# A hand-written order for four engines in branch A, gate copies staged in the weight tiles, and feed-forward weight sums issued after a result

## The chip, the cores and the metric

The kernel runs on one core of one Trainium2 chip. The metric is the device time of one execution in microseconds; a kernel's time is the median over its runs, and one more execution is recorded by the hardware profiler. TensorE does the matrix products (PE in the profile, PEld for its weight loads), VectorE is DVE, ScalarE is ACT, GpSimd is POOL and SyncE is SP, the engine that issues the transfers in the kernel before.

## The reference, cut to what matters

One encoder block over 1024 tokens and 16 meta tokens of width 1024, in float32. Branch A is differential attention (4 heads, two score maps each, over all 1040 keys), branch B is windowed attention; both are multiplied by a sigmoid gate, added, projected, and followed by a SwiGLU feed-forward.

```python
def diff_attn_rows(q1, q2, k1, k2, v, qpos, kpos, key_real, slopes, lam):
    ...
    s1 = jnp.einsum('bqhd,bkhd->bhqk', q1, k1).astype(jnp.float32) * scale + bias
    s2 = jnp.einsum('bqhd,bkhd->bhqk', q2, k2).astype(jnp.float32) * scale + bias
    attn = jax.nn.softmax(s1, axis=-1) - lam * jax.nn.softmax(s2, axis=-1)
    return jnp.einsum('bhqk,bkhe->bqhe', attn.astype(v.dtype), v)
...
    merged = jax.nn.sigmoid(ga) * (y_a @ w_ba) + jax.nn.sigmoid(gb) * (y_b @ w_bb)
    return merged @ w_o

def swiglu(h, w_gate, w_up, w_down):
    return (jax.nn.silu(h @ w_gate) * (h @ w_up)) @ w_down
```

## The kernel before, in words

**Products.** Every float32 product is made of three products of split operands: the operand is copied to a rounded high part (ACT, L113) and the rest is kept as a low part (L114, on DVE or POOL); TensorE then does high times high, high times low, low times high. The gates' projections, the output projection and the feed-forward are also done in seven block products instead of eight (blocks 1 to 7, `p` in the code), which takes sums of weight blocks and of results.

**The stage of branch A** (from 325 to 638 us). The outer loop at L926 runs over 32 tiles, `n`: 4 heads `h` of 8 tiles `t` of 128 queries. One tile's work is:

- `scores_a` (L813): for each of the two maps (m = 1, then 0) three chunks of keys (392, 392 and 256). TensorE makes the chunk in a PSUM bank (L829), DVE adds the distance bias and carries the running minimum (L832). After the third chunk ACT takes the exponential of the whole row and its sum (L837); DVE then takes a reciprocal (m = 1, L839) or a product of scalars (m = 0, L841), joins the two maps (L843) and copies 32 columns (L844).
- `transpose_a` (L847), for the tile before (T_LAG is 1): three groups of transposes (L855), each read by ACT (high part, L858) and DVE (low part, L859).
- `values_a` (L862) and `normed_a` (L872): the product with the values for each pair of tiles, and a norm for every four tiles.
- Between these, single steps of the gates' projection: `gate_steps` (L729) holds 50 products of four steps each, three matmuls a step (L738). A product's weights are loaded (`g_load`, L620) and split (`g_split`, ACT L113 and POOL L114). Its result goes from PSUM to DRAM: 26 products are copied by ACT to a staging tile (`gate_stage`, L746, two buffers), 24 (p in 1, 6, 7) are added by DVE to an earlier partial result that was loaded into a tile `gk` (L632, L743, three buffers). The store is L747.
- POOL forms sums of the output projection's weights (`wo_ahead`, L785), with loads and stores on SP.

Score chunks and transposes share five PSUM banks (tag "sc", SC = 5) in turn, the gate products two (PP2). The string `SLOTS` gives TensorE's order within a tile: s is a chunk of scores, g a gate step, t a group of transposes, n a step of values or norm. At the start of heads 1 to 3 ten gate steps stand together (G_HEAD), at the very start four, and 30 (HOLD) are kept for the end.

Inside `tc.manual_schedule(engines=...)` the named engines run instructions in the order in which the code writes them. In this stage only TensorE stands in such a block; the order of ACT, DVE, POOL and SP is chosen by the compiler's planner, which simulates the timeline beforehand. Once the program is built, each of these queues is fixed and runs in order.

**The feed-forward's first half** (from 808 to 1234 us). TensorE and DVE are in written order. A product `product_f` (L1456) is 12 matmuls (L1466). `prepare` (L1206) splits weights ahead of time, up to eight operand tiles; for block 6 the weights first need three sums on DVE (`weights`, L1247 to L1249). Results leave PSUM by ACT copies (L1486, L1489) or DVE operations (L1475, L1480, L1482). Four banks serve each of gate (i = 0) and up (i = 1) products; a product whose bank is still unread waits. `turn_f` (L1330) transposes the normed tokens and forms token sums (L1355 to L1358); `low_of` issues low parts that were put off (L1524).

Of the kernel before, what the change touches and what calls it, by code (L numbers as in the profile page):

```python
# [27 lines left out]
AH = 4  # L28
# [8 lines left out]
N_WAIT = 3  # L37
PP2 = 2
# [3 lines left out]
G_BUFS = 2  # L42
# [27 lines left out]
def encoder_block(ctx: ExitStack, tc: tile.TileContext, x, meta, norm_mix, w_in, lq1, lk1, lq2, lk2,  # L70
# [544 lines left out]
    def g_load(n, raw=None):  # L615
# [4 lines left out]
        nc.sync.dma_start(raw, ws_d[k][:, (5, 6, 7, 3).index(p)] if p in (5, 6, 7, 3) else  # L620
# [3 lines left out]
    def g_split(n, op=None):  # L624
# [9 lines left out]
    g_done = [0, 0]  # L634

    def g_ahead(n):
# [25 lines left out]
    def load_a0(h, q, k):  # L662
        q[0] = apool.tile([P, S], F32R, tag="q0", name=f"aq{h}_0")
        nc.sync.dma_start(f32(q[0]), qa_d[h][0])
        if h:
            load_k(h, 0, k[0])
            return q, k, load_v(h)
# [60 lines left out]

    def gate_steps():  # L729
        for n, (p, k) in enumerate(order_g):  # L730
            g_ahead(n + 1)
            op, act = g_ready.pop((p, k)), G_ACT[p]
# [3 lines left out]
            for c in range(4):  # L736
                for i, (a, b) in enumerate(((0, 0), (0, 1), (1, 0))):
                    nc.tensor.matmul(ps, op[:, a, c], quad(b, *act)[:, c], start=(p in (2, 5, 1) and c == 0 and i == 0),  # L738
                                     stop=(p in (2, 3, 4) and c == 3 and i == 2), skip_group_check=True)
                if c == 3:  # L740
                    if p in (1, 6, 7):
                        st = g_kept.pop((p, k))
                        nc.vector.tensor_tensor(st, ps, st, ALU.add)  # L743
                    else:
                        st = gpool.tile([P, 512], F32, tag="g", name="gate_stage", bufs=G_BUFS)
                        nc.scalar.copy(st, ps)  # L746
                    nc.sync.dma_start(g_place(p, k), st)  # L747
                    if (p, k) in ((5, 3), (5, 7), (3, 7)):
                        later_p = {(5, 3): 6, (5, 7): 7, (3, 7): 4}[p, k]
                        load_sums(later_p, *G_ACT[later_p])  # L750
# [9 lines left out]
    ld = *ld, load_v(0)  # L760
# [4 lines left out]
    prepool, close_pre = pool("prepool")  # L765
    wo_d = {(p, c): dram.tile([P, 512], F32, name=f"wo_d{p}_{c}") for p in (5, 6, 7, 3) for c in range(4)}
# [14 lines left out]
    def wo_ahead(n):  # L781
# [4 lines left out]
        nc.sync.dma_start(wo_d[(7, 5, 6, 3)[i], c], out)  # L786
# [26 lines left out]
    def scores_a(h, t, ld, s):  # L813
        slope = 2.0 ** -(2 * (h + 1))
        qs, ks, _ = ld
# [6 lines left out]
        u0 = 896 - t * P  # L822
        for m in (1, 0):
# [13 lines left out]
            nc.scalar.activation(s[m][:, 0:L], s[m][:, 0:L], AF.Exp, bias=low, scale=-1.0, accum_out=sum_of[m])  # L837
# [869 lines left out]
```

## Time and profile before

| | |
|---|---|
| median of 3 runs | 1450.66 us (1448.5 to 1454.46) |
| profiled execution: time, span | 1453.61 us, 1451.8 us |
| PE busy | 1419.5 us (98%) |
| PEld busy | 1216.4 us (84%) |
| DVE busy | 943.4 us (65%) |
| ACT busy | 696.0 us (48%) |
| POOL busy | 627.2 us (43%) |
| mean granted TensorE clock | 0.993 |

A row of a group of instructions gives line, engine, operation, the tiles it writes and reads, its shape and count, then busy time and the mean duration of one, then the engine's idle time just before such instructions and what ended it. A row of the timeline gives start and duration in us; in brackets is the engine's idle time before it and what ended that. A row of stages gives the length of a stretch, each engine's busy time in it with the count of instructions, the granted TensorE clock, the busy share of the DMA engines and GB/s. Matmuls overlap in their pipeline, so that one lasts longer than the distance to the next.

### The profile page before, as it was taken

What the parts mean: (1) busy time and instruction counts of PE and PEld (TensorE: products, weight loads), DVE (VectorE), ACT (ScalarE), POOL (GpSimd) and SP (SyncE); (2) the same over time, 40 slices, a digit from 0 to 9 for tenths busy, and PEclk for the clock granted to TensorE, in tenths of its full rate; (3) what the DMA queues carried; (4) which work ended last, traced back from release to release, by engine and by line L of the source; (5) the groups of instructions that cost most, each with busy time, mean ns of one, the idle gap of its engine ahead of it and who ended that gap; (6) DMA issues with size and microseconds to landing.
All of it is one profiled execution on the core that took longest, in us unless ns stands there. A gap on an engine that the chain in (4) does not pass through costs nothing. (4 is left out here: it accounts for less than half of the span.)

```text
span 1451.8 us, 21189 instructions
## 1 busy us (share of the span) xinstructions
PE 1419.5 (98%) x7231; PEld 1216.4 (84%) x7231; DVE 943.4 (65%) x1680; ACT 696.0 (48%) x1315; POOL 627.2 (43%) x593
## 2 busy tenths in 40 slices
PE   8999999998999899999999999999999999999997
PEld 7998989987888889888888878888888888888886
DVE  7478535637778788733876896554455554787567
ACT  6366535545555455555445633333333333444454
POOL 4599126743532122245144565454445452000444
PEclk9999999999999999999999999999999999999999
DMA  8467668988768564569522624333333333964443
GB/s 242 88 210 239 191 164 269 277 287 290 250 221 257 175 196 155 167 209 330 201 80 88 189 87 150 119 109 105 100 96 107 103 103 105 316 223 139 124 130 139
DMA packets 195804, 255.00 MB, mean 176 GB/s; under 512 B 18976, under 2 KB 116704, under 8 KB 195696
## 3 DMA queue, kind: packets, MB, share of 16 engines
q1 hardware_dynamic: 195696, 253.65, 55.6%
q8 instruction: 57, 0.93, 0.3%
q14 instruction: 51, 0.42, 0.1%
HBM read 165.84 MB, written 81.20 MB: 170 GB/s over the span
## 5 line engine op out<-in xcount | busy, mean ns | idle before, releaser
L114 POOL TENSOR_TENSOR wop<-wf,wop 128x512 fp32r<-128x512 f32 x128 | 175.1, 1372 | 167.8 <-ACT wop L113 155.3
L1466 PE MATMUL pg<-t,wop 128*128 128x512 f32 x1056 | 242.6, 389 | 0.0
L1466 PEld LDWEIGHTS pg<-t,wop 128*128 128x128 f32 x1056 | 198.3, 188 | 41.1
L1582 PE MATMUL pd<-ob,oa 128*128 128x512 f32 x924 | 210.4, 389 | 0.5 <-POOL oa L114 0.4
L1582 PEld LDWEIGHTS pd<-ob,oa 128*128 128x128 f32 x924 | 173.2, 188 | 37.6 <-POOL oa L114 0.9
L1466 PE MATMUL pg<-b,wop 128*128 128x512 f32 x792 | 185.2, 392 | 2.8 <-DVE copies_p L1480 2.8
L1466 PEld LDWEIGHTS pg<-b,wop 128*128 128x128 f32 x792 | 149.5, 189 | 34.2 <-DVE copies_p L1480 3.2
L738 PE MATMUL pg<-hT_hi,gop 128*128 128x512 f32 x384 | 144.4, 400 | 0.4 <-DVE gk L743 0.4
L114 POOL TENSOR_TENSOR gop<-gr,gop 128x512 fp32r<-128x512 f32 x47 | 64.4, 1373 | 165.7 <-ACT gop L113 161.3
L113 ACT ACTIVATE wop<-wf 128x512 fp32r<-128x512 f32 x128 | 80.1, 631 | 84.1 <-PE pg L1466 48.0
L114 POOL TENSOR_TENSOR oa<-ra,oa 128x512 fp32r<-128x512 f32 x33 | 44.1, 1337 | 170.6 <-ACT oa L113 169.2
L113 ACT ACTIVATE oa<-ra 128x512 fp32r<-128x512 f32 x77 | 48.7, 632 | 105.1 <-PE pd L1582 44.0
L837 ACT ACTIVATE as<-as,amn 128x1040 f32<-128x1040 f32 x64 | 74.5, 1164 | 49.9 <-DVE amn L832 41.4
L829 PE MATMUL aps<-ak,aq 128*128 128x392 f32 (+1 forms) x384 | 91.0, 331 | 7.1 <-DVE amn L832 6.2
L1247 DVE TENSOR_TENSOR s<-wf,wf 128x512 f32<-128x512 f32 x22 | 22.3, 1011 | 103.4 <-DMA wf<-in_w_ff_up_dram 52.3
L829 PEld LDWEIGHTS aps<-ak,aq 128*128 128x128 f32 x384 | 70.4, 192 | 21.0 <-DVE amn L832 7.5
L738 PEld LDWEIGHTS pg<-hT_hi,gop 128*128 128x128 f32 x384 | 73.3, 191 | 12.2 <-DVE gk L743 1.1
L339 POOL TENSOR_SCALAR bs<-bs,bdn 128x432 f32<-128x432 f32 (+1 forms) x64 | 41.4, 664 | 86.6 <-DVE bdn L337 74.3
L738 PE MATMUL pg<-hT_lo,gop 128*128 128x512 f32 x192 | 76.5, 398 | 0.0
L114 POOL TENSOR_TENSOR woh<-wo,woh 128x512 fp32r<-128x512 f32 x28 | 38.5, 1378 | 67.4 <-ACT woh L113 66.3
L329 DVE CUSTOM_DVE_ANT_0 bs<-bps,tbx,nsink 128x432 f32<-128x432 f32 (+1 forms) x64 | 38.2, 622 | 38.5 <-PE bps L327 29.3
L832 DVE CUSTOM_DVE_ANT_0 as<-aps,dist,far_a 128x392 f32<-128x392 f32 x64 | 39.6, 619 | 30.2 <-PE aps L829 29.7
(311 smaller groups left out, 3219.2 us busy)
## 6 DMA issues: line engine op xcount, KB each, us to landing
ra<-aop SPq DMA_DIRECT2D x77, 256.0 KB, 2.7
wf<-in_w_ff_gate_dram SPq DMA_DIRECT2D x24, 512.0 KB, 4.0
wf<-in_w_ff_up_dram SPq DMA_DIRECT2D x24, 512.0 KB, 3.9
aop<-as SPq DMA_DIRECT2D x44, 256.0 KB, 2.1
w_c<-in_w_in_dram SPq DMA_DIRECT2D x17, 512.0 KB, 5.9
aop<-c SPq DMA_DIRECT2D x33, 256.0 KB, 2.0
ts_d<-to SPq DMA_DIRECT2D x16, 512.0 KB, 3.6
gw<-in_w_in_dram SPq DMA_DIRECT2D x32, 256.0 KB, 4.2
```

Source lines behind the costliest of these rows:

```text
L113: nc.scalar.activation(hi, src, AF.Copy)
L114: lo_eng.tensor_tensor(lo, src, f32(hi), ALU.subtract)
L329: nc.vector.tensor_tensor_reduce(st[:, r, :W], ps[:, :W], tb, 2.0 ** -(4 * g + r + 1), nsink[:, 4 * g + r:4 * g + r + 1], ALU.add, ALU.min ...
L339: nc.gpsimd.tensor_scalar(st[:, r, :W], st[:, r, :W], dn[:, r:r + 1], 1.0, ALU.mult, ALU.mult)
L738: nc.tensor.matmul(ps, op[:, a, c], quad(b, *act)[:, c], start=(p in (2, 5, 1) and c == 0 and i == 0), stop=(p in (2, 3, 4) and c == 3 and ...
L829: nc.tensor.matmul(ps[:, :n], qs[m][:, t * P:(t + 1) * P], ks[m][:, vv, k0:k0 + n], start=(vv == 0), stop=(vv == 1))
L832: nc.vector.tensor_tensor_reduce(s[m][:, k0:k0 + n], ps[:, :n], far_by, slope, low, ALU.add, ALU.min, mn[:, m, i:i + 1])
L837: nc.scalar.activation(s[m][:, 0:L], s[m][:, 0:L], AF.Exp, bias=low, scale=-1.0, accum_out=sum_of[m])
L1247: tt(s1, a21, a22, ALU.add)
L1466: nc.tensor.matmul(ps, op[:, x, c, :], b[:, y, c, :], start=(p in (1, 2, 5) and c == 0 and n == 0), stop=(p in (4, 2, 3) and c == 3 and n ...
L1582: nc.tensor.matmul(ps[u], oa[:, a, u * P:(u + 1) * P], ob[:, b, :], start=(p in (1, 2, 5) and j == 0 and k == 0), stop=(p in (2, 3, 4) and ...
```

## The change

In branch A the loop is put inside a second `manual_schedule`, for ACT, DVE, POOL and SP, and the pieces of a tile's work are taken apart so that each stands at a written place:

- `exp_a`, `scale_a` and `join_a` are the exponentials, the reciprocal and the join, taken out of `scores_a`. The exponential of map 1 stands after the third chunk; that of map 0 after the first group of transposes (EXP_AT = 1). The join of a tile stands after the first chunk of the next tile; the copy of 32 columns and two of the three low parts of the transposes are put off (`behind`, `catch_up`) to just after that join and the second chunk.
- Splits of gate weights are put in a list (`held_back`) and let go one at a time (`let_go`) after the fifth chunk and after the third group of transposes.
- A gate result is not written at once: `settle` and `store_gates` issue it after the third or the sixth chunk, or at the second step of the next product. Stores of gate results and loads of gate weights are issued by ACT's queue (`nc.scalar.dma_start`) instead of SP's.
- Partial gate results are loaded by `ask_kept`, up to three ahead, apart from the splits.
- The staging tiles have three buffers (G_BUFS) in another pool, the first shares the tag "w", and the last two products' copies use weight tiles (tag "gr"). `yg` has one buffer instead of two.
- The next head's queries and keys are asked for in the last tile of a head, its values in its third tile.
- Tile 1 has two more gate steps; the loop's total count of gate steps is the same. `fill(1000)` is called before three pools are closed instead of after.

In the feed-forward `prepare` is not called before products 4 to 7 (it was: before 6 and 7), and is called right after product 7's results. In `turn_f` one token sum is formed from an ACT copy of a PSUM bank and the other PSUM bank instead of from two tiles in SBUF.

The diff, cut to its core:

```diff
-G_BUFS = 2
+G_BUFS = 3
...
-        nc.sync.dma_start(raw, ws_d[k][:, (5, 6, 7, 3).index(p)] if p in (5, 6, 7, 3) else
+        (nc.sync if held_back is None else nc.scalar).dma_start(raw, ws_d[k][:, (5, 6, 7, 3).index(p)] if p in (5, 6, 7, 3) else
...
         if p in (1, 6, 7):
-            kept = g_kept[p, k] = gpool.tile([P, 512], F32, tag="gk", name=f"gk{p}_{k}", bufs=GK_BUFS)
-            nc.sync.dma_start(kept, g_place(p, k))
+            kept_to_do.append((p, k))
+    def ask_kept():
+        while kept_to_do and len(g_kept) < GK_BUFS:
+            load_kept()
...
             while g_done[i] < min(n + far, len(order_g)):
-                what(g_done[i])
+                if i and held_back is not None:
+                    held_back.append(g_done[i])
+                else:
+                    what(g_done[i])
                 g_done[i] += 1
+    def let_go(n):
+        while n > 0 and held_back:
+            g_split(held_back.pop(0))
+            n -= 1
...
+    def gate_result(p, k, ps):
+        if p in (1, 6, 7):
+            while (p, k) not in g_kept:
+                load_kept()
+            st = g_kept.pop((p, k))
+            nc.vector.tensor_tensor(st, ps, st, ALU.add)
+        else:
+            tag, bufs = ("w", 2) if (p, k) == order_g[0] else ("g", G_BUFS)
+            if (p, k) in order_g[-2:]:
+                st = gpool.tile([P, 512], F32, tag="gr", name=f"gate_stage{p}_{k}", bufs=GR_BUFS)
+            else:
+                st = prepool.tile([P, 512], F32, tag=tag, name=f"gate_stage{p}_{k}", bufs=bufs)
+            nc.scalar.copy(st, ps)
+        to_store.append((p, k, st))
...
+    def store_gates():
+        while to_store:
+            p, k, st = to_store.pop(0)
+            nc.scalar.dma_start(g_place(p, k), st)
+    def settle(store=True):
+        while owed:
+            gate_result(*owed.pop(0))
+        if store:
+            store_gates()
...
+                if c == 1 or burst[0]:
+                    settle()
+                if c == 1:
+                    ask_kept()
                 if c == 3:
...
+                    owed.append((p, k, ps))
...
+    def exp_a(s, m):
+        sum_of, dn = s["of"]
+        nc.scalar.activation(s[m][:, 0:L], s[m][:, 0:L], AF.Exp, bias=s["low", m], scale=-1.0, accum_out=sum_of[m])
...
+        behind[1:1] = [lambda: nc.vector.tensor_copy(s[0][:, L:L + 2 * NM].rearrange("p (a k) -> p a k", a=2),
+                                                     s[0][:, S:L].unsqueeze(1).broadcast_to([P, 2, NM]))]
...
+    order_av = tc.manual_schedule(engines={mybir.EngineType.Activation, mybir.EngineType.DVE, mybir.EngineType.Pool, mybir.EngineType.SP})
+    order_av.__enter__()
...
+        for what in SLOTS if n != 1 else "sgsgsngsgssggtntnt":
+            if what == "s" and n < AH * NT:
+                next(scoring)
+                scored += 1
+                if scored == 1 and n:
+                    join_a(tiles[n - 1][2])
+                    catch_up(1)
+                if scored == 2:
+                    catch_up(9)
+                if scored == 3:
+                    exp_a(s, 1)
+                    settle()
+                    if t == NT - 1 and h < AH - 1:
+                        ask_kept()
+                        ahead = load_a1(h + 1)
+                    if n == 0:
+                        let_go(1)
+                if scored == 4 and t in (3, 4, 5, 6):
+                    wo_ahead(4 * h + t - 3)
+                if scored == 5:
+                    scale_a(t, s)
+                    if n:
+                        let_go(1)
+                if scored == 6:
+                    settle(False)
+                if scored == 6 and n == 0:
+                    exp_a(s, 0)
+                    store_gates()
+                if scored == 6 and t == NT - 1 and h < AH - 1:
+                    ahead = load_a0(h + 1, *ahead)
+            elif what == "t" and n:
+                next(turning)
+                turned += 1
+                if turned == EXP_AT and n < AH * NT:
+                    exp_a(s, 0)
+                    store_gates()
+                if turned == 3:
+                    let_go(1)
...
-        nc.vector.tensor_tensor(left, t2, left, ALU.subtract)
+        nc.scalar.copy(left, pts[1])
+        nc.vector.tensor_tensor(left, left, pts[0], ALU.subtract)
...
-        if n not in (4, 5):
+        if n not in range(4, 8):
             prepare()
...
         product_f(*steps[n][1])
         used[0] -= 1
+        if n == 7:
+            prepare()
         low_of(2)
```

More of the change, by code (lines that the diff above doesn't have):

```diff
@@ L37 @@
 N_WAIT = 3
+EXP_AT = 1
 PP2 = 2
@@ L739, in gate_steps @@
                                      stop=(p in (2, 3, 4) and c == 3 and i == 2), skip_group_check=True)
+                if c == 1 or burst[0]:
+                    settle()
+                if c == 1:
+                    ask_kept()
                 if c == 3:
[L741 to L750, printed above, removed]
+                    owed.append((p, k, ps))
+                    if n == len(order_g) - 1:
+                        settle()
                 yield
@@ L978, in encoder_block @@
     close_pre()
+    fill(1000)
     close_apool3()
```

108 lines of the change are left out of this document (72 added, 36 removed).

## The prediction

> **What bounds the kernel now.** I read the page's busy times first, then the stages, then TensorE's waits in the two stages that the change touches, then the stretches at a lower clock.
>
> ```profile
> span 1451.8 us, 21189 instructions
> PE 1419.5 (98%) x7231; PEld 1216.4 (84%) x7231; DVE 943.4 (65%) x1680; ACT 696.0 (48%) x1315; POOL 627.2 (43%) x593
> ```
> ```profile
> 325.00:638.40 313.40, 298.59 (x1768) 266.52 (x1767) 239.41 (x664) 173.21 (x324) 97.68 (x77) 0.98 0.64 210
> ...
> 808.40:1233.80 425.40, 422.64 (x1868) 349.81 (x1866) 254.93 (x280) 165.93 (x288) 215.94 (x156) 1.00 0.36 113
> ```
> ```profile
> PE aps L829 <- DVE amn L832: 6.2, 4, 2.2
> PE apt L855 <- DVE as L843: 4.4, 5, 2.0
> ```
> ```profile
> PE pg L1466 <- DVE copies_p L1480: 2.8, 1, 2.8
> ```
> ```profile
> 341.38:344.80 3.42, 3.42 (x13) 3.13 (x12) 3.27 (x14) 2.58 (x6) 2.74 (x3) 0.50 1.07 405
> ...
> 843.14:846.55 3.41, 3.32 (x8) 2.65 (x9) 3.41 (x4) 1.49 (x3) 3.41 (x3) 0.50 0.00 0
> ```
>
> TensorE bounds the kernel: it is busy 98% of the span, and the change adds and removes no matmul. So all that can be won is TensorE's own idle time. In the stage of branch A (first row of stages) that is 313.40 - 298.59 = 14.8 us, most of it behind DVE: score chunks that wait for a bank DVE has not read, and transposes that wait for the join. In the feed-forward's first half it is 425.40 - 422.64 = 2.8 us, one single wait for a bank (L1480). The last fence holds the first and last of four stretches with a granted clock of 0.50, each 3.41 or 3.42 us long; three lie in branch A and one in the feed-forward, each at or behind the end of a long wait. Half a clock for 3.42 us costs 1.7 us of work, so 5.1 us and 1.7 us. What the change could win at most is 14.8 + 5.1 = 19.9 us in branch A and 2.8 + 1.7 = 4.5 us in the feed-forward: 24.4 us, or 1.7%.
>
> Here a rule and the trace differ. The Trainium skill ("TensorE: Matmul & The Clock Gate", section "Why this matters for your kernels") says that idle gaps beyond about 3 us put the clock back to half. The longest waits here are 2.2, 2.0 and 2.8 us (last column of the three rows of waits), and yet half clock followed. By the page's rule the 6.8 us would have some other cause and stay; that case is among the rivals.
>
> **Branch A: what blocks, and what the written order does to it.**
>
> ```profile
> 336.24 0.16 DVE L839 RECIPROCAL adn<-adn 128x1 f32<-128x1 f32 x1 [4.48 <-ACT as L837]
> ```
> ```profile
> 403.38 0.59 ACT L746 COPY gate_stage<-pg 128x512 f32<-128x512 f32 x1 [3.46 <-DMA g_d<-gate_stage]
> ```
> ```profile
> 405.15 0.16 DVE L839 RECIPROCAL adn<-adn 128x1 f32<-128x1 f32 x1 [3.75 <-ACT as L837]
> ...
> 406.05 0.48 DVE L832 CUSTOM_DVE_ANT_0 as<-aps,dist_m,amn 128x256 f32<-128x256 f32 x1
> ```
> ```profile
> 479.27 0.69 DVE L743 TENSOR_TENSOR gk<-pg,gk 128x512 f32<-128x512 f32 x1 [2.18 <-DMA gk<-g_d]
> ```
>
> Each of the three clock losses has a queue that stood still. At 336.24 DVE waited 4.48 us for an exponential, at 405.15 it waited 3.75 us for one, because ACT's queue held a gate copy in front that waited 3.46 us for a store to free its staging tile. At 479.27 DVE stood 2.18 us in front of a partial gate result that had not been loaded. DVE's score chunks stood behind each, and TensorE behind those. The change puts the exponential of map 1 ahead of the gate copy and of the split, gives staging three buffers, and asks for partial results up to three ahead. I cost these three blocks at nothing afterwards: the cover is a store or load that now has three products (three tiles, some 22 us) to land. In the ten gate steps ahead of a head three products take only about 8 us; if a load misses there, DVE stands about 2 us as at 479.27.
>
> What comes in their place is a chain. In the written order these stand in line, each behind the one before on its engine or for its data: the last chunk of map 1 on DVE, the exponential on ACT, a split, the high part of the first transposes, the second exponential, then on DVE the scalar product, the join, a low part, a chunk, the 32-column copy, another low part, and the last chunk of map 1 of the next tile. The planner could put other work between; now one turn of this loop is the least time of a tile.
>
> ```profile
> 488.27 1.16 ACT L837 ACTIVATE as<-as,amn 128x1040 f32<-128x1040 f32 x1 [0.28 <-DVE amn L832]
> 489.34 0.19 ACT L837 ACTIVATION_READ_ACCUMULATOR as<-as,amn 128x1 f32 x1
> 489.43 0.58 ACT L858 ACTIVATE at<-apt 128x512 fp32r<-128x512 f32 x1
> 489.90 0.59 ACT L875 ACTIVATE ysq<-apy 128x512 f32<-128x512 f32 x1
> ...
> 493.93 0.58 ACT L746 COPY gate_stage<-pg 128x512 f32<-128x512 f32 x1 [2.69 <-PE pg L738]
> 494.41 0.63 ACT L113 ACTIVATE gop<-gr 128x512 fp32r<-128x512 f32 x1
> 494.94 1.15 ACT L837 ACTIVATE as<-as,amn 128x1040 f32<-128x1040 f32 x1
> ```
> ```profile
> 489.56 0.27 DVE L841 TENSOR_SCALAR adn<-adn,neglam,as 128x1 f32<-128x1 f32 x1 [0.72 <-ACT as L837]
> 489.86 1.30 DVE L843 SCALAR_TENSOR_TENSOR as<-as,adn,as 128x1040 f32<-128x1040 f32 x1
> 491.08 0.62 DVE L832 CUSTOM_DVE_ANT_0 as<-aps,dist,far_a 128x392 f32<-128x392 f32 x1
> 491.63 0.08 DVE L832 DVE_READ_ACCUMULATOR2_ANT amn<- 128x1 f32 x1
> 491.63 0.69 DVE L859 TENSOR_TENSOR at<-apt,at 128x512 fp32r<-128x512 f32 x1
> 492.23 0.17 DVE L844 COPY as<-as 128x32 f32<-128x32 f32 x1
> 492.31 0.27 DVE L859 TENSOR_TENSOR at<-apt,at 16x128 fp32r<-16x128 f32 x1
> 492.51 0.60 DVE L832 CUSTOM_DVE_ANT_0 as<-aps,dist,amn 128x392 f32<-128x392 f32 x1
> ```
> ```profile
> 489.50:526.20 36.70, 13.97 (x60) 10.80 (x60) 16.62 (x30) 1.00 0.39 126
> ```
>
> From start to start in these rows: last chunk 0.48 (the row at 406.05), exponential 1.16, split 0.53, high part 0.47, second exponential to scalar product 1.29, scalar product 0.30, join 1.22, chunk 0.55, low part 0.60, copy 0.08, low part 0.20: 6.88 us. The norm's three small DVE instructions, once in four tiles and each at most a low part's 0.60, add up to 0.4 a tile: 7.3 us. Where the gate result is an ACT copy (0.48 in the rows), 7.8 us. Against it stands TensorE's own pace: the last row counts the score matmuls of a stretch with hardly a wait, 60 at 12 a tile, so 5 tiles in 36.7 us or 7.34 us a tile. DVE-gate tiles fit, tiles with an ACT copy miss by 0.4 us.
>
> The issue of transfers on ACT has no row, since ACT issues none before. SP's rows for the same store take this:
>
> ```profile
> 494.54 0.34 SPq L747 DMA_DIRECT2D g_d<-gate_stage  x1
> ```
>
> The lower bound is nothing (the queue issues while ACT works, and SP's shorter queue even helps). The upper bound is a store and a load at 0.34 each, behind the full 0.58 of the copy instead of 0.48: 0.8 us a tile, where both stand between the two exponentials. By the written positions that is so in heads 0 and 2, where a product ends at a tile's second gate step; after the ten extra steps of heads 1 and 3 it ends at the fourth, and the store falls behind the second exponential.
>
> The tiles: with ACT copies 6 in head 0, 5 in head 1, and a quarter of 14 in heads 2 and 3 (products of block 4), 14.5 in all. Lower end 14.5 x 0.42 = 6 us. Upper end: head 0 6 x 1.2 = 7.2, head 1 2.1, head 2 (a quarter at 1.2, the rest at 0.2) 2.9, head 3 0.7: 13 us. I take the middle, 9.5 us, because half of the tiles stand where the issue has no cover. Refilling the chain in tiles 0 and 1 and behind each head I put at 2.5 us (four times about the 0.6 us of one low part that arrives late). Sum for branch A: 19.9 goes, 12 comes, 7.9 us won. Single waits of the new kind are around a microsecond, under the 2 us and more behind which this trace lost clock.
>
> Other moved steps: the loads of the next head go out in the last tile, some 5 us sooner on SP, but behind `ask_kept`, which may hold SP for a store's landing; the values go out two tiles later and are wanted a tile after that. Stores and weight loads leave SP, so nothing of SP's queue is lengthened. The `wo` sums and norms are in POOL's queue between splits; POOL is busy 98 of 313 us here and covers them. The two extra gate steps in tile 1 come off the end: no matmul more. `fill(1000)` and the pools' closing move no instruction of TensorE.
>
> **The feed-forward.**
>
> ```profile
> 836.10 0.68 DVE L1247 TENSOR_TENSOR s<-wf,wf 128x512 f32<-128x512 f32 x1
> ...
> 839.71 1.65 DVE L1249 TENSOR_TENSOR wf<-s,wf 128x512 f32<-128x512 f32 x1
> 841.29 1.28 DVE L1524 TENSOR_TENSOR t<-ts,t 128x512 fp32r<-128x512 f32 x2
> 842.49 0.68 DVE L1480 TENSOR_TENSOR copies_p<-pg,copies_p 128x512 f32<-128x512 f32 x1
> ```
>
> Six sums run on DVE from 836.10 to 841.29, and product 7's result (L1480), for whose bank TensorE waits, runs behind them at 842.49. Without them in front it runs at about 842.49 - 5.2 = 837.3; the bank is wanted at 843.23 - 2.76 = 840.5. So this wait and its clock loss go. Next in line are the sums themselves: behind L1480 and L1482 (at most another 1.65) they begin at about 839.6, the first three end near 841.7, and ACT and POOL need 0.6 and 1.3 for the split: 843.6, when product 12 wants it one product (2.7 us) behind 840.5, at 843.2, and its low part 0.4 later. The second block of three is as tight. I leave 1.2 us there, so 3.3 of 4.5 us are won; the ends are 0 and 4.5. The ACT copy in `turn_f` is 4 x 0.6 us on an engine with room; DVE's part loses one SBUF operand, which I count as nothing.
>
> **The sum.** 7.9 + 3.3 = 11.2 us. The profiled execution took 1453.61 us, 1.8 beyond its span; it would take 1442.4. It lies 2.95 us above the median of 1450.66, so the median would be 1439.5. I say 1440.
>
> **Rivals.**
>
> 1. Nearly all is won: ACT's issue is free and the chain has slack, so that 4 us stay in branch A and none in the feed-forward. 1450.7 - 15.9 - 4.5 = 1430. For it: DVE stands still no longer than these blocks. Against: the sum of the chain.
> 2. The wait only changes its place: upper end of the chain (13), 5 us of refilling at four heads, and the weight sums late by as much as they gain (1 us won). 1450.7 - 1.9 - 1 = 1448. The page's rule on the clock lands here too: with the 6.8 us left in place 4.4 us are won, 1446; four half-clock stretches behind four waits speak against it, chance 0.02, counted in this case.
> 3. Slower. The store and the load on ACT's queue cost their 0.8 us in every tile, with the copy's 0.42, because in-order ACT stands at each issue wherever it is written: 31 x 1.2 = 37 us come, 19.9 + 3.3 go, 1465. It decides from 0.98 us a tile on (30 us against the 23 won and 7 of the bound). Against it: half of the stores stand behind the second exponential, off the chain, and DVE's gates need no copy.
>
> **How the numbers follow.** About 0.5%, 7 us, is what a measurement of this kernel can tell from no change. My forecast has 0.45, rival 1 0.15, rival 2 0.28, rival 3 0.12. Faster is the first two, 0.60; same 0.28; slower 0.12. The range runs from just below rival 1 to beyond rival 2, 1428 to 1453, and leaves out rival 3 and a little on either side. The forecast's own range, 6 to 13 us in the chain and 0 to 4.5 in the feed-forward, is 1435 to 1446.
>
> **What would show it.** In TensorE's waits of branch A the three long ones and their half-clock stretches are gone; what is left is many waits of 0.3 to 1.2 us on DVE, more in head 0 than in head 3. ACT's exponential of map 1 starts within 0.1 us of its chunk, and the wait before the scalar product L841 ("ACT as") grows, since DVE now stands for the second exponential. In the feed-forward L1480 of product 7 runs ahead of L1247, and the 2.8 us wait is gone or is a shorter one for a split weight. I am wrong if ACT's issues show as gaps between the two exponentials in all tiles (rival 3), if a new wait near 2 us halves the clock again, or if a head's first chunk waits for its keys behind `ask_kept`.

## The result: about 1% slower

The changed kernel takes 1466.52 us (median of 9 runs, 1460.58 to 1472.29) against 1450.7 us for the kernel before (median of 9 runs on the same chip, the three shown among them). The ratio is 1.0097, 95% interval 1.0073 to 1.0122. The forecast was 1440, with 1453 as the upper end of the range; what came is on the other side. The profiled execution was the fastest of the nine, 1460.58 us.

The page's busy times (span 1458.8 us, 21151 instructions), then the two stretches at half clock, and branch A and the feed-forward's first half as rows of stages (columns as in the prediction):

```profile
PE 1420.5 (97%) x7231; PEld 1210.3 (83%) x7231; DVE 934.4 (64%) x1680; ACT 693.4 (48%) x1319; POOL 630.3 (43%) x593
```
```profile
831.71:835.12 3.41, 3.41 (x9) 2.63 (x8) 3.31 (x5) 1.46 (x3) 3.41 (x3) 0.50 0.47 161
473.31:483.55 10.24, 5.34 (x15) 4.24 (x16) 2.03 (x6) 1.33 (x4) 2.51 (x2) 0.50 0.42 135
323.10:643.70 320.60, 301.56 (x1769) 262.24 (x1768) 234.12 (x664) 168.57 (x324) 100.91 (x77) 0.98 0.63 204
815.10:1240.70 425.60, 422.68 (x1865) 349.75 (x1866) 251.91 (x279) 166.81 (x289) 213.89 (x156) 1.00 0.36 113
```

TensorE does the same 7231 matmuls. Branch A takes 320.60 us where it took 313.40, and TensorE's idle time in it is 19.0 us where it was 14.8. The feed-forward has not changed (425.60 against 425.40), so the step that was to win 3.3 us there won nothing. In this execution the three half-clock stretches of branch A are gone, as forecast, but one of 10.24 us has come, in which TensorE works 5.34 us; at half clock that is 2.7 us lost. TensorE's waits in the two stages (who waited for whom: total us, times, longest):

```profile
PE aps L888 <- DVE at L934: 8.0, 11, 1.2
PE pg L790 <- ACT gop L114: 6.8, 1, 6.8
...
PE pg L790 <- ACT gate_stage L762: 1.9, 1, 1.9
...
PE aps L888 <- DVE amn L891: 1.5, 4, 0.5
```
```profile
PE pg L1593 <- DVE kept L1484: 2.9, 1, 2.9
PE pg L1593 <- ACT kept L1483: 1.2, 1, 1.2
```

The first row is the chain of the prediction, many waits of up to 1.2 us behind low parts (L934). The second is new and single: the gate product at the start of head 2 waits 6.8 us for a split of its weights. The third is of the same kind, at head 1: a gate product waits 1.9 us for ACT to copy an earlier result out of its bank. The last two are the feed-forward's: the wait for L1480 is gone and the edit in `turn_f` has put two others in its place.

What stood behind the 6.8 us is read from ACT's, DVE's and SP's queues in that place (time line; ACTq and SPq rows are issues of transfers):

```profile
463.30 1.47 ACTq L621 DMA_DIRECT2D gr<-in_w_in_dram  x2
...
472.23 1.16 ACT L901 ACTIVATE as<-as,amn 128x1040 f32<-128x1040 f32 x1 [9.54 <-DMA gr<-in_w_in_dram]
...
476.51 0.35 ACTq L771 DMA_DIRECT2D g_d<-gk  x1
476.95 0.39 ACTq L621 DMA_DIRECT2D gr<-in_w_in_dram  x1
477.39 1.15 ACT L114 ACTIVATE gop<-gr 128x512 fp32r<-128x512 f32 x2 [3.90 <-DVE gk L755]
```
```profile
475.79 0.69 DVE L755 TENSOR_TENSOR gk<-pg,gk 128x512 f32<-128x512 f32 x1 [3.59 <-DMA gk<-g_d]
```
```profile
471.17 2.93 SPq L643 DMA_DIRECT2D gk<-g_d  x2
```

Read it from the end. TensorE needs the split at 477.39. It stands behind the store at 476.51, which stores what DVE adds at 475.79, and that sum waited 3.59 us for a partial result, whose load SP issued as late as 471.17. All of ACT's queue stood there for a store that belongs to DVE. (The 9.54 us in the row at 472.23 are no such hold: by DVE's rows the exponential's own last chunk ended at 472.20.) That ACT would stop is what the prediction did not cost: it gave an issue a price (0.34 us), not a wait.

### The profile page after: what moved, and what is told of

Same layout as the page of the kernel before. It is cut to its first block, busy times and chain, and to the rows that moved or that the text cites. A ratio compares the mean times of both kernels' runs of the same rounds, so it can differ in the third digit from the quotient of the medians.

```text
span 1458.8 us, 21151 instructions
## 1 busy us (share of the span) xinstructions
PE 1420.5 (97%) x7231; PEld 1210.3 (83%) x7231; DVE 934.4 (64%) x1680; ACT 693.4 (48%) x1319; POOL 630.3 (43%) x593
## 4 chain that ended last, share of the span: by engine, by line
PE 73%; DVE 6%; DMA 6%; POOL 5%; issue 5%; ACT 3%; ACTq 1%; SPq 0%; POOLq 0%; DVEq 0%
PE pg L1593 28%; PE pd L1711 8%; PE pg L790 6%; PE aps L888 3%; PE pp_qb L211 3%; PE po_x L1314 3%; PE ppa L866 3%; POOL oa L115 3%; PE pp_ka L211 2%; PE pp_va L211 2%; PE apy L947 2%; PE pp_qa L211 2%; PE po_y L1314 1%; DMA ak<-ka_d 1%; DMA gt<-g_d 1%
## 5 line engine op out<-in xcount | busy, mean ns | idle before, releaser
L934 DVE TENSOR_TENSOR at<-apt,at 128x512 fp32r<-128x512 f32 (+1 forms) x96 | 52.4, 548 | 26.4 <-ACT at L932 24.2
```

The lines of the kernel that those rows point to most:

```text
L934: nc.vector.tensor_tensor(lo, pt[:lo.shape[0], :nb], f32(hi)[:lo.shape[0]], ALU.subtract)
```

## The experiments

First a second profile, and the parts by themselves.

**The changed kernel again.**

> The changed kernel once more, for a second profile: the profiled execution of the first was the fastest of its nine runs (1460.58 us, median 1466.52). If the loss sits where that profile has it (a wait of 6.8 us for a gate split at the start of head 2 with 10 us of half clock behind it, waits of 8.0 us for low parts, 4.1 us in the feed-forward), the same three stand in this one, and a slower execution has a second long wait at the start of another head. If the loss is spread over every tile, the waits for low parts grow instead and the long wait stays one.

1465.49 us, ratio 1.0101 [1.0084, 1.0117]; the profiled span is 1465.4 us. TensorE's waits in branch A:

```profile
PE pg L790 <- ACT gop L114: 8.8, 1, 8.8
```

The same waits stand in the same places, the long one longer and those for low parts 6.8 us; no second long one at another head. The clock differs: besides the 10.24 us at head 2, from 476.79 on, two stretches of 3.41 us at 0.50 are back in branch A, from 381.22 and from 401.70. From the first score chunk to the last transposes of a norm this execution takes 315.35 us, the kernel before 304.47 (row further on).

**Gate transfers back on SP.**

```diff
-        (nc.sync if held_back is None else nc.scalar).dma_start(raw, ws_d[k]...
+        nc.sync.dma_start(raw, ws_d[k]...
...
-            nc.scalar.dma_start(g_place(p, k), st)
+            nc.sync.dma_start(g_place(p, k), st)
```

> Loads of gate weights and stores of gate results are issued by SP instead of ACT; all else as in the changed kernel. Theory: each of these issues on ACT waits for an earlier transfer to land (the next head's keys and queries among them), and ACT's exponentials and splits stand behind it. Then the wait of 6.8 us for the split at head 2 and the 5.1 us that its half clock costs go or shrink, 8 to 12 us off the changed kernel: 1455 to 1459. Rival, the partial gate result that DVE waits for is late by itself: the split is early, but DVE still stands until the load lands, a wait of 3 to 4 us stays and at most 5 us go. Rival, the chain of every tile alone: the issue costs 0.8 us in 14.5 tiles at most, nothing changes at the head, and the waits for low parts fall from 8.0 to near 0.

1456.32 us, ratio 1.0039 [1.0024, 1.0054]: 9 to 10 us of the loss come from the place from which these transfers are issued.

```profile
PE aps L888 <- DMA ak<-ka_d: 4.7, 4, 1.5
PE pg L790 <- ACT gop L114: 2.9, 1, 2.9
...
PE aps L888 <- DVE at L934: 1.2, 4, 0.5
```

Both theories hold a part: the wait at head 2 falls from 6.8 and 8.8 to 2.9, and the waits for low parts from 8.0 and 6.8 to 1.2. What comes is 4.7 us for keys (`ak`), whose loads now share SP's queue with gate stores. (The 5.1 us that the expectation gave to half clock was half of 10.24; the loss is 2.7, since TensorE stood for the rest.)

**The feed-forward's two edits.**

```diff
-        nc.scalar.copy(left, pts[1])
-        nc.vector.tensor_tensor(left, left, pts[0], ALU.subtract)
+        nc.vector.tensor_tensor(left, t2, left, ALU.subtract)
```

> The changed kernel with the old token sum in the feed-forward (from two tiles in SBUF, no ACT copy of a bank). Theory: the two waits of 1.2 and 2.9 us for the bank that the new form holds until ACT and DVE have read it, and the 1.7 us of half clock behind them, are that form's price: 4 to 6 us off the changed kernel, about 1461, and no wait of its kind in the profile. Rival, the sums of weights put behind a result are late: a wait of the same size stays at product 7 or 12, and the time stays at 1466.

1462.27 us, ratio 1.0083 [1.0066, 1.0101], against the changed kernel's 1.0101 [1.0084, 1.0117]: about 3 us less, but the intervals overlap. The two waits of 2.9 and 1.2 us are not in its profile, but the rival's is, 2.6 us for L1606 (L1607 of the changed kernel, L1480 before). The other edit alone, on the kernel before:

```diff
-        if n not in (4, 5):
+        if n not in range(4, 8):
             prepare()
...
         used[0] -= 1
+        if n == 7:
+            prepare()
```

> The kernel before with one part of the change: the splits of weights are not prepared ahead of products 4 to 7 but once behind product 7. Theory (the prediction's step for the feed-forward): the wait of 2.8 us and its 1.7 us of half clock go, 1.2 us comes, so 3.3 us (0 to 4.5) off the kernel before, 1447. Rival, the sums are late by as much as they gain: a wait of 1 to 3 us stands at product 12, the time stays at 1450.

1453.21 us, ratio 1.0008 [0.9993, 1.0024]: nothing won. The wait for L1480 is as long as before, but it is for another L1480 (waits of the feed-forward, then of the merge of the branches, then DVE's time line):

```profile
PE pg L1466 <- DVE copies_p L1480: 2.6, 1, 2.6
```
```profile
PE po_x L1188 <- DVE gt L1164: 3.4, 2, 2.1
```
```profile
852.83 2.87 DVE L1524 TENSOR_TENSOR t<-kept,t 128x512 fp32r<-128x512 f32 x2
855.62 3.45 DVE L1253 TENSOR_TENSOR wf<-wf,wf 128x512 f32<-128x512 f32 x2
859.00 0.68 DVE L1480 TENSOR_TENSOR copies_p<-pg,copies_p 128x512 f32<-128x512 f32 x1
```

No bracket stands in these rows: DVE is never idle. The sums were put behind product 7's result, and all that follows moved back, so that product 11's result is late instead. Where an engine works without a gap, an order of its work chooses which wait it makes.

**Where on ACT: heads or tiles.** A flag `in_head` is true for the ten steps ahead of a head and for that head's first tile (and behind the last tile), and chooses SP there:

```diff
-            nc.scalar.dma_start(g_place(p, k), st)
+            (nc.sync if in_head[0] else nc.scalar).dma_start(g_place(p, k), st)
...
+                burst[0] = in_head[0] = True
...
+            if t == 1:
+                in_head[0] = False
```

and the same choice for the loads; in the counterpart it is `not in_head[0]`.

> The changed kernel, but SP issues the gate loads and stores written in the ten steps ahead of a head and in that head's first tile; in the other tiles ACT issues them as in the change. Theory (ACT's queue is held where these issues wait behind the next head's keys and queries): the wait for the split at head 2 falls from 8 us to 3 or less and its half clock goes, while the waits for low parts in the other tiles (6.8 to 8.0 us) stay: 1457 to 1460. Rival (ACT's issue costs its time in every tile, heads included): little changes, 1463 or more.

> The reverse: SP issues the gate loads and stores of all tiles but a head's first, ACT those of the ten steps ahead of a head and of its first tile. Theory: the waits for low parts fall from 6.8 to 8.0 us to about 1 us (as with all issues on SP), the wait at head 2 stays at 7 to 9 us with its half clock: 1460 to 1462. Rival (issue costs in every tile decide): most of the 10 us that moving all issues gave comes from here, 1457 or less.

Heads on SP: 1457.74 us, 1.0046 [1.0029, 1.0062]. Tiles on SP: 1474.47 us, 1.0159 [1.0141, 1.0177], slower than the change itself, which neither theory had. TensorE's waits of the first, then of the second, and one row each of DVE and ACT in the second:

```profile
PE aps L888 <- DVE at L934: 7.7, 10, 1.2
PE pg L790 <- ACT gop L114: 2.9, 1, 2.9
```
```profile
PE pg L790 <- ACT gop L114: 10.6, 1, 10.6
PE aps L888 <- DMA ak<-ka_d: 9.7, 6, 2.5
...
PE aps L888 <- DVE at L934: 0.7, 3, 0.2
```
```profile
477.02 0.07 DVE L891 DVE_READ_ACCUMULATOR2_ANT amn<- 128x1 f32 x1
```
```profile
478.70 1.16 ACT L901 ACTIVATE as<-as,amn 128x1040 f32<-128x1040 f32 x1 [11.24 <-DMA ak<-ka_d]
```

By the waits the two losses come apart: issues on ACT at the heads make the long wait, issues on ACT in the tiles make the waits for low parts. By the time they do not weigh the same: with the heads alone on SP (1457.74) the kernel is nearly where it is with all on SP (1456.32), since the tiles' transfers on SP bring waits for keys in their place (4.7 us with all on SP, 9.7 with the tiles alone).

The last two rows must be read together. The exponential at head 2 is put down to a landing of keys, after 11.24 us, but its own last chunk ended at 477.09, so the transfers held it for the last 1.6 us only. The semaphore events show how they did. The landings of SP's and ACT's transfers raise the same eight semaphores in rotation, and an issue first waits until the transfer that last used its semaphore has landed. So gate transfers on ACT waited for keys that SP had asked for: here the issue ahead of the exponential, at 478.31, for a landing of keys at 478.24; in the changed kernel the issue at 463.30 for one at 463.22. SP's own queue is tied in the same way: the load of the partial result, at 471.17 in the changed kernel, waited for the last of the keys, which landed at 471.15. With the tiles' transfers on SP the last of the keys took 13.9 us from issue to landing (10.0 in the changed kernel); DVE's sum at head 2 then waited 7.4 us for its partial result (3.59), and ACT's store and split stood behind it.

The 1.9 us at head 1 are the plainest case: in the changed kernel ACT's copy at 398.84 stood behind issues at 395.95 and 398.42, which waited for landings of head 1's queries and keys at 395.87 and 398.34.

**Stores or loads.** The same flag for one kind alone.

> The changed kernel, but of the gate transfers written in the ten steps ahead of a head and in its first tile the stores alone go to SP; the loads stay on ACT. With both on SP the wait for the split at head 2 was 2.9 us and no half clock, with both on ACT 6.8 and 8.8 us. Theory A, the stores hold ACT (one waits 3.5 us for DVE's sum, which waits for a partial result): the wait falls to 3 to 5 us, about 1458 to 1460. Theory B, the loads hold it (their issue waits for the landing of the next head's keys): the wait stays at 6 us or more, 1463 or more.

> The counterpart: in those places the loads go to SP and the stores stay on ACT. Theory A: the wait stays at 6 us or more, 1463 or more. Theory B: it falls to 3 to 5 us, 1458 to 1460. If both this and the run before stay near 1465, either kind alone holds ACT to the same landing.

Head stores on SP: 1457.39 us, 1.0036 [1.0024, 1.0049], a wait of 2.8 us. Head loads on SP: 1459.37 us, 1.0049 [1.0031, 1.0067], a wait of 7.1 us:

```profile
PE pg L790 <- ACT gop L114: 2.8, 1, 2.8
```
```profile
PE pg L790 <- ACT gop L114: 7.1, 1, 7.1
```

(The expectation was wrong in one thing: behind the 2.9 us with heads on SP the clock is 0.50 for 3.4 us.) Theory A by the waits: the stores hold ACT. By the times it is less clear, since the second kernel's 1459.37 falls in theory B's bounds and its interval meets the first's; its profile is of the slowest of seven runs, 1464.21. Then all stores on SP and all loads on ACT, which leaves the tiles to judge:

> The changed kernel with all stores of gate results on SP and all loads of gate weights on ACT. Which of the two kinds delays the chain in every tile (the waits for low parts, 7 to 8 us with both on ACT, about 1 us with both on SP)? If the stores, which stand right behind an exponential in the written order: about 1 us here. If the loads: 6 us or more. At head 2 the wait for the split is 2.9 us. Time 1455 to 1458.

1458.16 us, 1.0045 [1.0024, 1.0065], and most of the waits for low parts are gone:

```profile
PE aps L888 <- DMA ak<-ka_d: 5.6, 3, 3.1
...
PE aps L888 <- DVE at L934: 1.2, 4, 0.5
```

So the stores on ACT made the waits for low parts as well. The time did not fall below that of the kernel with the heads' stores alone on SP (1457.39): 5.6 us of waits for keys came instead. The changed kernel's ACT rows in a tile show what the store did:

```profile
362.58 0.56 ACT L762 COPY gate_stage<-pg 128x512 f32<-128x512 f32 x1
363.18 0.33 ACTq L771 DMA_DIRECT2D g_d<-gate_stage  x1
363.54 0.45 ACTq L621 DMA_DIRECT2D gr<-ws_d  x1
364.03 0.63 ACT L114 ACTIVATE gop<-gr 128x512 fp32r<-128x512 f32 x1 [0.89 <-ACT gate_stage L762]
```

The store must wait for the end of the copy, and the load stands behind the store; ACT is idle for 0.89 us between the two exponentials. With the stores on SP the load of the same tile is issued at 361.56, while the first exponential still runs, and ACT has no gap there.

**Without the next heads' keys.**

```diff
-                        ahead = load_a1(h + 1)
+                        ahead = ld
...
-                    ahead = load_a0(h + 1, *ahead)
+                    ahead = ld
```

> The changed kernel with all its transfers on ACT as they are, but the queries and keys of heads 1 to 3 are not loaded: these heads use head 0's (left out: 9 MB of loads, three times 3 MB). Theory (ACT is held by the landing of those loads): the 6.8 to 8.8 us wait at head 2 goes, with its 5 us of half clock, and the waits for low parts stay near 7 us: about 1453. Rival (issues on ACT and the partial results hold it by themselves): a wait of 4 us or more stays at head 2, 1460 or more.

1456.43 us, 1.0036 [1.0021, 1.005], with all gate transfers on ACT; between the two expectations. The wait at head 2 is 3.2 us, the one at head 1 is gone, the waits for low parts are 7.7. So the landing of the queries and keys is what held ACT for 4 to 6 us; about 3 us stay in every kernel in which that split is written behind the head's first exponential.

**A mended order.** All gate transfers on SP and the old feed-forward; then two moves at the heads:

> The changed kernel with all gate loads and stores issued by SP, and the feed-forward as it was before (old token sum, weights prepared before products 6 and 7). Theory: branch A is now 0 to 3 us better than before, the feed-forward the same: 1449 to 1453. Rival: the written order of four engines costs something that the waits of TensorE do not show, and the time stays at 1456.

1455.02 us, 1.0031 [1.0016, 1.0046]: 1.3 us off the kernel with the new feed-forward, between the two expectations and not clear of the noise.

```diff
+                    if t == NT - 1 and h < AH - 1:
+                        ahead = load_a1(h + 1)
                     settle()
                     if t == NT - 1 and h < AH - 1:
                         ask_kept()
-                        ahead = load_a1(h + 1)
...
             g_ahead(n + 1)
+            let_go(early[0])
+            early[0] = 0
```

(`early[0]` is 1 at the first gate product ahead of heads 1 to 3.)

> The kernel of the run before this, with two moves at the heads: in the last tile the next head's first queries and keys are asked for ahead of the gate stores and partial results, and one split of gate weights is let go at the first product of the ten steps. Theory: the wait for the split at head 2 (2.9 us) and most of the waits for keys (4.7 us) go, 4 to 7 us off: 1445 to 1449. Rival: the keys' landing is bound by the transfers' bandwidth, which a few us of earlier issue don't change; then only the split's wait goes, 1450.

1450.34 us, 1.0000 [0.9986, 1.0015]. The split's wait is gone and the keys' waits are down from 5.2 to 1.8 us (the kernel of 1455.02, then this one):

```profile
PE aps L888 <- DMA ak<-ka_d: 5.2, 5, 1.8
```
```profile
PE pg L792 <- ACT gate_stage L762: 2.0, 1, 2.0
...
PE aps L890 <- DMA ak<-ka_d: 1.8, 2, 1.0
```

These waits went as the theory says, 4.7 us off, but the time is the kernel before's, the rival's number. A new wait took back 2.0 us: at head 1 ACT now stands in front of the early split until its weights land, at 391.35, and the copy of a result for whose bank TensorE waits stands behind it. From the first score chunk to the last transposes of a norm (rows of stages: the kernel before, the same again in another execution, the changed kernel, this one):

```profile
327.54:632.01 304.47, 289.66 (x1729) 259.27 (x1728) 238.03 (x662) 172.03 (x322) 96.84 (x77) 0.98 0.64 211
```
```profile
326.04:628.04 302.00, 287.99 (x1730) 256.36 (x1729) 238.70 (x662) 171.78 (x322) 98.39 (x77) 0.99 0.65 213
```
```profile
325.86:637.38 311.52, 292.48 (x1730) 254.82 (x1729) 232.74 (x662) 165.72 (x319) 97.05 (x74) 0.98 0.63 205
```
```profile
327.26:627.72 300.46, 290.84 (x1730) 254.15 (x1729) 232.22 (x662) 165.60 (x321) 96.26 (x76) 0.99 0.66 214
```

Branch A is 1.5 to 4 us shorter than in the kernel before; the kernel before itself differs by 2.5 us between two executions. The second execution of the kernel before is this run:

> The kernel before once more, for a second profile. Its first shows the merge of the branches with a wait of 0.5 us for the gated product; the other kernels show 0.4 to 2.1 us there, and half clock behind some. If that wait changes from execution to execution, it is another here, and branch A's idle time again 13 to 17 us with two or three half-clock stretches; if it belongs to the change, it is 0.5 us again.

1451.35 us; the wait in the merge is 1.0 us, after 0.5 in the first execution and 3.4 (the row of L1188) in the kernel with one edit in the feed-forward. The edit in the feed-forward lies behind the merge, and in that kernel DVE, ACT, POOL and SP do the same work there in the same order as in the kernel before. So that stage changes by itself, and the mended kernel's profile has 2.1 us there. Half clock changes too: this second execution has one stretch of it in branch A, from 340.97, where the first had three.

**The feed-forward with work taken off DVE.** On the mended kernel: first with the weights behind product 7 and block 7's low parts on POOL, then with the weights as before and those of block 5 too.

```diff
-        if p == 4:
+        if p in (4, 7):
             nc.gpsimd.tensor_tensor(lo, src, f32(hi), ALU.subtract)
```

> The kernel with all gate transfers on SP and the two moves at the heads (1450.34 us), with the feed-forward's weights prepared behind product 7 as in the change, and the low parts of block 7's token sums on POOL instead of DVE. Theory (DVE has no idle time around products 4 to 12, so that an order of its work only moves the wait, while work taken from it removes it): the 2.8 us wait for a product's bank and its 1.7 us of half clock go, 3 to 4.5 us off: 1446 to 1447. Rival (POOL, at about twice DVE's time for such an operation, brings its low parts late): a wait for a low part of 1 to 3 us in place of it, 1450.

> The kernel with all gate transfers on SP, the two moves at the heads and the feed-forward's weights prepared as before, with the low parts of blocks 5 and 7 of the token sums on POOL (block 7 alone, and weights behind product 7, left two waits of 0.9 and 1.1 us for split weights and 3.4 us of half clock). Theory (DVE has no idle time there): with eight operations less in front of it the six sums and product 7's result come in time, no wait over 0.5 us and no half clock at products 7 to 12: 1445 to 1447. Rival: the feed-forward's waits are not what separates this kernel from a gain, because another stage (the merge of the branches) gives the time back; the profile shows the wait gone and the time stays at 1450.

The first takes 1450.71 us, 0.9990 [0.9974, 1.0006]; the second 1455.95, 1.0035 [1.0019, 1.0052]. TensorE's feed-forward waits of the first and of the second:

```profile
PE pg L1595 <- POOL wop L115: 1.1, 1, 1.1
PE pg L1595 <- ACT wop L114: 0.9, 1, 0.9
```
```profile
PE pg L1595 <- DVE copies_p L1609: 6.1, 1, 6.1
```

In the first the wait for a result is gone and the split weights are late, behind which the clock is halved for 3.4 us once more. The second fails for a reason that neither expectation had. Two of the six sums of weights in the mended kernel with POOL's row beside the second, then one in this kernel with POOL's row:

```profile
835.53 0.69 DVE L1377 TENSOR_TENSOR wf<-wf 128x512 f32<-128x512 f32 x1
...
838.36 1.66 DVE L1378 TENSOR_TENSOR wf<-s,wf 128x512 f32<-128x512 f32 x1
```
```profile
837.74 1.73 POOL L115 TENSOR_TENSOR wop<-wf,wop 128x512 fp32r<-128x512 f32 x1 [3.45 <-ACT wop L114]
```
```profile
833.17 1.61 DVE L1377 TENSOR_TENSOR wf<-wf 128x512 f32<-128x512 f32 x1
```
```profile
832.49 3.44 POOL L1651 TENSOR_TENSOR t<-kept,t 128x512 fp32r<-128x512 f32 x2
```

Beside a POOL that works on tiles in SBUF, DVE's operation takes 1.6 us instead of 0.69. In the mended kernel that happens to the last of the six alone, here to all six, 831.30 to 841.52, and product 7's result comes behind them. Work handed to POOL slowed what stayed.

**The mended kernel with loads on ACT.** The last kernel, with the loads as in the change:

> The kernel of the first run of this call, but with the loads of gate weights on ACT's queue, as in the change. Theory: with the stores off it ACT is not held, and SP's queue is free of loads, so the keys' waits (1 to 2 us) go as well: 1444 to 1447, the same as or a little below the first run. Rival: ACT's loads wait for the landing of the keys too and hold the exponential at a head, or keep the low parts' waits: 1450 or more.

1456.36 us, 1.0037 [1.0021, 1.0054]; it carries the same 6.1 us in the feed-forward, so its time can't decide between the expectations. Beside the kernel of 1455.95, from which it differs in the loads alone, it is the same. Its branch A has no wait for a split, 1.2 us for low parts and 2.2 for keys: loads on ACT do no harm there.

## Why the prediction was wrong, by its steps

**What goes (19.9 us in branch A).** Half right. The blocks of 4.48 and 3.46 us are not in the new profile. The third, DVE in front of a partial result that has not been loaded, stands at head 2 again, 3.59 us where it was 2.18. The three half-clock stretches were in part chance: the kernel before has one in its second execution, and the changed kernel, which has none of them in its first, has two in its second.

**The chain in every tile (9.5 us taken, and 2.5 for refilling).** The size came out, by luck: the waits of TensorE behind DVE come to 8.0 + 1.5 = 9.5 us, and the copy, store and load between the two exponentials cost 0.89 us against a bound of 0.8. It was put down above all to the length of the chain, 6 us with issues that cost nothing. The run with all gate transfers on SP has 1.2 and 1.9 us for the same two rows of waits, and the runs with the stores alone on SP have 1.2 us for low parts too: it is the store on ACT. (In the upper end head 2's share comes to 3.2 us by its own terms, not 2.9; the 13 us stand.)

**"I cost these three blocks at nothing afterwards."** This step failed, and the wait of the third block is the one that it left in. It allowed that a load might miss in the steps ahead of a head, "DVE stands about 2 us". DVE stood 3.59 us, but behind it stood the store in ACT's queue, and behind that the split. TensorE waited 6.8 us (8.8 in the second profile) and lost 2.7 more at half clock: 9.5 us where 2 were allowed for a single engine. Of the wait, four to six us came from the stores on ACT, the rest from a split written behind the head's first exponential. The cover that it counted, three products to land in, about 8 us at a head, did not hold: SP could not issue the load of the partial result before the last of the keys had landed, at 471.15. In medians, all gate transfers back on SP took 1466.52 to 1456.32, the old feed-forward 1455.02, two moves at the heads 1450.34.

**The issue on ACT, between nothing and 0.8 us a tile.** The same failure seen from the term of the sum: SP's row gave the duration of an issue, 0.34 us, and what an issue waits for was left out. On SP a held store delays transfers; on ACT it delays exponentials and splits. That "nothing of SP's queue is lengthened" was beside the point.

**The feed-forward (3.3 us won).** Failed twice. The sums' order: L1480 of product 7 does run first, but the next late thing was not the split weights (1.2 us), it was the result of product 11, 2.6 us, because DVE has no gap there. Only the half clock is gone. And `turn_f`, "an engine with room": ACT's copy of the bank ran late, and DVE and then TensorE stood for it:

```profile
828.98 0.63 ACT L114 ACTIVATE wop<-wf 128x512 fp32r<-128x512 f32 x1 [1.06 <-DMA wf<-in_w_ff_up_dram]
829.51 0.57 ACT L1483 COPY kept<-ptn_f 128x512 f32<-128x512 f32 x1
```
```profile
830.11 0.69 DVE L1484 TENSOR_TENSOR kept<-kept,ptn_f 128x512 f32<-128x512 f32 x1 [3.28 <-ACT kept L1483]
```

The old form read both banks early and summed in SBUF; the new one keeps a bank until ACT has come round to it, behind splits that wait for loads. An engine that is busy 39% of a stage can still be late.

**The rivals.** The third named the number (1465) and half of the cause, in-order ACT standing at its issues, but in every tile by duration; the larger part is the heads, by waiting, so that its number agrees is luck. Its condition (0.98 us a tile) was nearly met by the 0.89 us, yet most tiles have slack. The second had the feed-forward right: late by as much as was gained.

**The clock.** That waits of the new kind would not halve it held in the first profile alone. In the second, half clock follows a wait of 0.92 us that ends at 379.06 (from 381.22 on) and one of 2.04 us that ends at 401.06 (from 401.70 on); the first has waits of 0.91 and 1.87 us in the same places, and no half clock behind them. So one of the prediction's own signs of being wrong came, a new wait near 2 us that halves the clock. The Trainium skill ("TensorE: Matmul & The Clock Gate", section "Why this matters for your kernels") puts the limit at idle gaps beyond about 3 us. Here half clock follows a single wait of 2.92 us (row 831.71), but none follows the 2.64 us in the kernel with the weights alone moved (clock 1.00 from 859.70 to 863.10), and it follows two waits of 0.9 and 1.1 us within 2 us. The length of one wait does not decide it, in these runs.

**What stays open.** Why no version is clearly faster than the kernel before. Profiles of the mended kernels with gate transfers on SP have branch A at 297.39 to 300.90 us against 302.00 and 304.47; the medians do not follow, 1450.34 and 1450.71 at best. Waits in the merge that come and go by 1 to 3 us, and half clock that comes and goes by 1.7 us a stretch, hide gains of that size in a single profile. What brings the half clock on is open too.

## What to carry to other kernels

Before moving a transfer to another engine's queue, ask what its issue waits for and who stands behind it there: a store belongs on a queue where nothing critical is behind it. Even the engine that had made the data, ACT with its copies in the tiles, stood 0.89 us for its own store and the load behind it. A wait moved on an engine without gaps appears one result later; look for the next late result, not only for the operand that was moved. A single profile of a 1% change can be the fastest run: take a second one.

## What the runs showed of the hardware

Issues by two engines are tied to each other through the semaphores of their landings: ACT's issue at 463.30 and SP's at 471.17 each followed, by 0.08 and 0.02 us, the landing of keys that SP had asked for. Half clock in these stages comes in stretches of 3.41 us or two and three times that (6.83, 10.24), and the same wait is followed by one in one execution and by none in another. And DVE's 0.69 us for an operation of 128x512 in SBUF becomes 1.6 to 1.8 us while POOL works in SBUF as well.
